# Key norms inside the last projection, transposes first in the chain, and level masks written one level ahead, in a hybrid decoder step

## The chip, the cores and the metric

The kernel runs on one core of a Trainium2 chip. The metric is the device time of one execution in microseconds (us). The kernel before took 2987.66, 2988.45 and 2995.47 us in three runs; the median is 2988.45 us.

One core has five engines that work side by side, each of them strictly in the order in which its own instructions stand: PE (matrix products), DVE and POOL (elementwise work), ACT (activations and copies) and SP, which issues most transfers. An engine that waits for another one holds up everything that stands behind the waiting instruction on it.

## The reference

The program computes one step of a decoder layer over 2048 prompt tokens (with 16 learned tokens ahead of them) and 32 sampling tokens: a layer norm, one projection for two groups of heads, an output projection, and a dense feed-forward net. Four heads are retention heads, four are gated DeltaNet heads. The change lies in the second kind. For each chunk of 128 tokens and each head the reference computes:

```python
gk = l2_norm(silu(conv(...)))                       # keys
G = jnp.cumsum(g, axis=-1)
decay = jnp.exp(jnp.where(incl, G[..., :, None] - G[..., None, :], -jnp.inf))
kk = jnp.einsum('bnhid,bnhjd->bnhij', k, k)
lower = jnp.where(strict, kk * decay, 0.0) * beta[..., :, None]
a_mat = jnp.eye(C, dtype=q.dtype) + lower
sol = lax.linalg.triangular_solve(a_mat, rhs, left_side=True, lower=True, unit_diagonal=True)
attn = jnp.einsum('bnhid,bnhjd->bnhij', q, k) * decay

def step(s, xs):                                    # over the chunks
    wv, wk, at, qg, kt, cd = xs
    u = wv - jnp.einsum('bhcd,bhde->bhce', wk, s)
    o = jnp.einsum('bhcd,bhde->bhce', qg, s) + jnp.einsum('bhij,bhje->bhie', at, u)
    s = cd[..., None, None] * s + jnp.einsum('bhcd,bhce->bhde', kt, u)
    return s, o
```

## The kernel before

The program has three stages one after the other: the mixers of both kinds of heads (`attention`, the first 1310 us or so of the profile), the output projection, and the feed-forward net. The change touches the first stage alone.

**Blocks and heads.** The tokens are worked in four blocks b0 to b3 of four chunks of 128 tokens. Block b0 also has a fifth, short tile, with the learned tokens and the sampling tokens. In each block the eight heads follow in the order r0 g0 r1 g1 r2 g2 r3 g3 (b3: r0 g0 g1 r1 g2 g3 r2 r3), with r a retention head and g a gated DeltaNet head. For each head a projection runs (`ret_proj` or `gdn_proj`): products on PE at line L406, out of `wh`, `wl` (weights, split in a high and a low part) and `xT`, into PSUM tiles `pj`, of which there are two. Behind it the head's chain (`ret_chain` or `gdn_chain`, which calls `gdn_group`) is begun, and its steps are laid between the products of the projections that follow: `advance(us)` is called with the time of each piece of a projection, and takes as many steps of the chain as the list `LAT` and `pace` say. A `yield LAT[i]` in the chain is such a step's end. From what is written in this way, the framework's tile scheduler puts the instructions of each engine in their final order.

**A retention projection** gives q and k of a chunk into one `pj` tile. DVE multiplies it by the rotation's cosines and sines (`qk`, L571, and `rotB`, L572), POOL adds the two (L573, into `qk`), and DVE scales the keys (`rkd`, L634), out of what POOL has added.

**A gated DeltaNet projection** has four parts (q, k, v and the gate), of which each is followed by its short convolution (`cacc`, L862). `flip(a)` (L805 to L820) transposes q or k, takes the square sums of its rows on ACT, and for k leaves the transposed keys in `kp`. Both come in the sixth piece of a part's products: q's in the k part's, k's in the gate part's. The norms' reciprocal square roots and the scale factors `gsk` come when the projection is over.

**The chain of a gated DeltaNet head** (`gdn_group`) begins with the decays: `mg` on DVE (L918), products `pe` with a triangle of ones on PE (L921), the exponential `E` on ACT (L925), and its strict and its inclusive triangle on POOL, `Es` (L926, in `mg`'s buffer, and so named `mg` in the views) and `E` (L927). Then the keys are scaled by `gsk` on DVE (`kp`, L935), v is transposed and scaled (`vb`, L938 and L939), the scaled keys are transposed on PE (L943) and copied by ACT to `kT` (L945), and keys times keys (L949, called kT·kT here) give `LT` on DVE (L951), which is `Es` times that product. From `LT` the triangular matrix is inverted over seven levels: DVE makes the first level's masked matrix `Z` (L960) and `U` (L961), POOL makes the other six, `Lm` (L963), one instruction for each level; then come six rounds of products (L973, L980, L982), each of which uses one slice of `Lm`, and a refinement (L993, L1001). Last comes the scan over the chunks: the products with the state, kS and qS (L1035, L1036), `r` on DVE (L1038), `Vr` on PE (L1043), `ku` (L1052), the state's update on DVE (`S_gdn`, L1053), for which the next chunk's kS waits, and the output `O` (L1055). In b0 a second, small chain (called the side chain here) runs for the short tile between the steps of the first.

**What sets the order.** While the chain of head h runs its inversion, the scan of the same block's previous gated DeltaNet head, which `advance` carries under the key "h", and the retention projection that follows in the head order lie on the same engines. Heads 1 and 2 of a block also have the layer norm of the next block's tokens beside them (`xa` at L307 on DVE and at L309 on POOL).

The lines of the chain's first part, up to the end of the masks, are the ones that the change rewrites:

```python
nc.gpsimd.tensor_tensor(out=Es, in0=E, in1=bc(ST), op=ALU.mult)          # L926
nc.gpsimd.tensor_tensor(out=E, in0=E, in1=bc(M1), op=ALU.mult)           # L927
nc.vector.tensor_tensor(out=kp, in0=kp, in1=lane(sk[:R, 1, here]), op=ALU.mult)   # L935
for x in range(1, nl):
    nc.gpsimd.tensor_tensor(out=Lm[:, x - 1], in0=LT, in1=lvl(x), op=ALU.mult)    # L963
```

Of the kernel before, what the change touches and what calls it, by code (L numbers as in the profile page):

```python
# [239 lines left out]
class Builder:  # L240
# [547 lines left out]
    def gdn_proj(self, b, h, G, out):  # L788
        nc, mp, cp = self.nc, self.mp, self.cvp
        xh, xl = self.xT  # L790
        T = CPB * 128 + (SP if b == 0 else 0)
# [81 lines left out]
        rn = self.rsqrt(sq.rearrange("p a b -> p (a b)"), 2 * nt, 128, self.sm, 1.0, 4.0 * RMS_EPS).rearrange("p (a b) -> p a b", a=2)  # L873
        sk = self.sm.tile([128, 2, nt], F32, tag="gsk", name="gsk")
        nc.vector.tensor_scalar(out=sk[:, 0], in0=rn[:, 0], scalar1=HD ** -0.5, scalar2=None, op0=ALU.mult)
        nc.vector.tensor_tensor(out=sk[:, 1], in0=rn[:, 1], in1=G["sb"][:, :, h], op=ALU.mult)
        out += [cv, zg, sk, kps]
# [20 lines left out]
    def gdn_group(self, b, h, cv, zg, sk, kp, G, mixd, ts, tiles):  # L898
# [21 lines left out]
        for i in range(m):  # L920
            nc.tensor.matmul(pe[:R, i, :R], lhsT=U1, rhs=mg[:, i, :], start=True, stop=True)  # L921
# [6 lines left out]


        kp = kp[:R]  # L930
        vb = big("vb", 2, n=128)[:R]
        lane = lambda a: a.unsqueeze(2).broadcast_to([R, m, 128])
        here = slice(ts[0], ts[0] + m)
        cq = sk[:R, 0, here]
        nc.vector.tensor_tensor(out=kp, in0=kp, in1=lane(sk[:R, 1, here]), op=ALU.mult)  # L935
        p = wide()[:R, :m, :]
        for i in range(m):
            nc.tensor.transpose(p[:, i, :], v[:, col(i):col(i) + R], self.ident)  # L938
        nc.vector.tensor_tensor(out=vb, in0=p, in1=lane(G["sv"][:R, here, h]), op=ALU.mult)  # L939
        yield LAT[7]  # L940
        pk = wide()
        for i in range(m):
            nc.tensor.transpose(pk[:, i, :R], kp[:, i, :], idn)  # L943
        kT = big("kT", 2)[:, :, :R]
        nc.scalar.copy(out=kT, in_=pk[:, 0:m, :R])  # L945
        yield LAT[8]
# [15 lines left out]
        for x in range(1, nl):  # L962
            nc.gpsimd.tensor_tensor(out=Lm[:, x - 1], in0=LT, in1=lvl(x), op=ALU.mult)  # L963
# [695 lines left out]
```

## Time and profile before

| | |
|---|---|
| median of three runs | 2988.45 us (2987.66 to 2995.47) |
| the profiled execution's own time | 2991.86 us |
| span of its instructions | 2990.1 us |
| clock that PE was granted, mean | 0.982 of full speed |
| share of the span that PE is busy | 96% |
| first stage (mixers) | 0 to about 1310 us |
| output projection and feed-forward net | about 1310 us to the end |

The profile shows one execution. "Busy" is the time that an engine's instructions take in the records. A row of grouped instructions gives the line, the engine, the operation, output and inputs with their sizes, the count, then the busy time and the mean nanoseconds of one, and last the idle time just before them with what ended it. A row of waits gives the engine and the line that waited, what it waited for, the total in us, the count, and the longest one. A row of the timeline gives the start in us, the duration, the engine and the line, and in brackets the idle time ahead of it with what ended it. A row of windows gives the stretch and its length, then the busy time (and count) of PE, PE's weight loads, DVE, ACT and POOL, the granted clock, the share of DMA, and GB/s.

### The profile page before, as it was taken

Reading aid. Unit: us, or ns where it says so; the run is one execution under the profiler, and the core shown is the slowest. Engines: PE = TensorE matmul, PEld = TensorE weight load, DVE = VectorE, ACT = ScalarE, POOL = GpSimd, SP = SyncE. Lnnn points to the kernel's source line nnn. Section 1 sums busy time; section 2 is a strip of 40 time slices with the busy share of each in tenths; the row PEclk is TensorE's granted clock in tenths of the full one; section 3 lists DMA queues with packets and bytes.
Section 4 is the critical chain, followed back from the end, with each engine's and each line's share of the span. In section 5 each row is a group of like instructions: output and inputs, shape, how many; then the busy total and the mean of one; then the engine's idle time right before and its main releaser. Section 6 shows DMA issues by size and latency. Waiting matters only on the chain.

```text
span 2990.1 us, 47480 instructions
## 1 busy us (share of the span) xinstructions
PE 2862.8 (96%) x17942; PEld 2554.7 (85%) x17942; DVE 1934.2 (65%) x4205; ACT 996.2 (33%) x2351; POOL 782.9 (26%) x759
## 2 busy tenths in 40 slices
PE   6999999999999999998998999999999999999997
PEld 6877888888888878877777999999999999989895
DVE  7767677776776676657776766667544444844456
ACT  2434343444444444432233333333211112321121
POOL 1312222221222122225544434433200111411111
PEclk8989999999999999999999999999999999999998
DMA  7543534444344333356658766667755555787762
GB/s 258 202 169 142 205 134 152 148 170 152 150 157 156 135 121 122 125 157 228 218 184 286 281 223 228 228 234 260 274 183 184 176 184 184 272 295 238 240 227 85
DMA packets 223093, 580.89 MB, mean 194 GB/s; under 512 B 27296, under 2 KB 62672, under 8 KB 206480
## 3 DMA queue, kind: packets, MB, share of 16 engines
q1 hardware_dynamic: 222864, 577.86, 55.6%
q8 instruction: 141, 2.31, 0.3%
q14 instruction: 88, 0.72, 0.1%
HBM read 409.48 MB, written 168.30 MB: 193 GB/s over the span
## 4 chain that ended last, share of the span: by engine, by line
PE 78%; DVE 13%; DMA 3%; ACT 3%; issue 2%; POOL 1%; SPq 0%; POOLq 0%; ACTq 0%; DVEq 0%
PE d L406 20%; PE pj L406 19%; PE Y L406 8%; PE X L406 8%; PE Z L406 8%; PE W L406 4%; DVE cacc L862 1%; ACT junk L813 1%; PE w L980 1%; DMA bd<-spare 1%; PE rt L668 1%; PE w L973 1%; DMA fr<-bd 1%; PE w L982 1%; PE rt L641 1%
## 5 line engine op out<-in xcount | busy, mean ns | idle before, releaser
L406 PE MATMUL pj<-wh,xT 128*128 128x256 f32 (+2 forms) x2176 | 459.7, 295 | 7.6 <-ACT wh L349 3.7
L406 PE MATMUL pj<-xT,wh 128*128 128x512 f32 (+1 forms) x1280 | 379.7, 381 | 1.8 <-ACT cpre L846 1.0
L406 PEld LDWEIGHTS pj<-wh,xT 128*128 128x128 f32 (+1 forms) x2176 | 353.7, 188 | 12.9 <-ACT wh L349 4.0
L1506 DVE TENSOR_TENSOR y<-y,d 128x512 f32<-128x512 f32 (+1 forms) x344 | 235.2, 684 | 173.6 <-PE d L406 173.5
L406 PE MATMUL pj<-wl,xT 128*128 128x256 f32 (+3 forms) x1088 | 310.6, 286 | 0.5 <-POOL wl L356 0.5
L406 PE MATMUL d<-dh,fh 128*128 128x512 f32 (+1 forms) x745 | 297.4, 399 | 10.1 <-DVE y L1504 6.5
L406 PE MATMUL d<-dh,fl 128*128 128x512 f32 (+1 forms) x745 | 295.5, 397 | 0.0
L406 PE MATMUL d<-dl,fh 128*128 128x512 f32 (+1 forms) x745 | 294.1, 395 | 0.8 <-DVE dl L356 0.8
L356 POOL TENSOR_TENSOR fl<-ta,fh 128x384 fp32r<-128x384 f32 (+1 forms) x65 | 63.8, 981 | 748.7 <-issue 541.5
L406 PEld LDWEIGHTS pj<-xT,wh 128*128 128x128 f32 x1280 | 211.9, 194 | 25.1 <-issue 3.4
L406 PE MATMUL pj<-xT,wl 128*128 128x512 f32 (+1 forms) x640 | 229.7, 359 | 0.0
L406 PEld LDWEIGHTS pj<-wl,xT 128*128 128x128 f32 (+1 forms) x1088 | 205.1, 188 | 1.0 <-POOL wl L356 0.8
L406 PEld LDWEIGHTS d<-dh,fl 128*128 128x128 f32 (+1 forms) x745 | 137.3, 184 | 38.3 <-issue 0.5
L406 PEld LDWEIGHTS d<-dh,fh 128*128 128x128 f32 (+1 forms) x745 | 137.6, 185 | 29.8 <-DVE y L1504 7.1
L406 PEld LDWEIGHTS d<-dl,fh 128*128 128x128 f32 (+1 forms) x745 | 137.5, 185 | 20.6 <-DVE dl L356 1.1
L406 PEld LDWEIGHTS pj<-xT,wl 128*128 128x128 f32 x640 | 122.7, 192 | 16.8 <-issue 0.8
L862 DVE SCALAR_TENSOR_TENSOR cacc<-cpre,cw,cacc 128x512 f32<-128x512 f32 (+1 forms) x144 | 115.9, 805 | 31.9 <-ACT cacc L860 30.4
L963 POOL TENSOR_TENSOR Lm<-LT,lvl 128x512 f16<-128x512 f32 (+1 forms) x108 | 129.2, 1228 | 11.3 <-DVE LT L951 10.5
L1405 DVE TENSOR_TENSOR u<-x,Y 128x384 f32<-128x384 f32 (+1 forms) x132 | 67.6, 512 | 96.3 <-PE Y L406 95.8
L349 ACT CAST fh<-ta 128x384 fp32r<-128x384 f32 (+1 forms) x66 | 31.8, 482 | 289.7 <-DVE ta L1413 289.7
L406 PE MATMUL X<-b,a12h 128*128 128x384 f32 (+1 forms) x528 | 126.2, 325 | 0.4 <-ACT x L1419 0.4
L406 PE MATMUL X<-b,a11h 128*128 128x384 f32 (+1 forms) x528 | 124.7, 321 | 0.0
(391 smaller groups left out, 7170.9 us busy)
## 6 DMA issues: line engine op xcount, KB each, us to landing
wh<-parts SPq DMA_DIRECT2D x45, 1024.0 KB, 5.5
wl<-parts SPq DMA_DIRECT2D x45, 1024.0 KB, 6.8
fr<-dn SPq DMA_DIRECT2D x66, 512.0 KB, 5.6
fr<-gu SPq DMA_DIRECT2D x44, 512.0 KB, 4.9
s12h<-wd SPq DMA_DIRECT2D x44, 512.0 KB, 4.8
s12l<-wd SPq DMA_DIRECT2D x44, 512.0 KB, 5.8
s34h<-wd SPq DMA_DIRECT2D x44, 512.0 KB, 3.8
s34l<-wd SPq DMA_DIRECT2D x44, 512.0 KB, 4.8
```

Of the source, the lines that this page charges most:

```text
L349: i = nc.scalar.copy(out=h, in_=src)
L356: i = (nc.vector if el == "dve" else nc.gpsimd).tensor_tensor(out=l, in0=src, in1=h.bitcast(F32), op=ALU.subtract)
L406: self.nc.tensor.matmul(out, lhsT=a(k), rhs=b(k), start=first and k == 0 and i == 0, stop=last and k == kn - 1 and i == 2, skip_group_chec ...
L641: nc.tensor.matmul(pp[:rows, 2, :rows], lhsT=kT, rhs=qT, start=True, stop=True)
L668: nc.tensor.matmul(po, lhsT=sc, rhs=v, start=True, stop=False)
L813: nc.scalar.activation(out=junk, in_=p[:, j, :], func=AF.Square, accum_out=sq[:, a, t:t + 1])
L862: nc.vector.scalar_tensor_tensor(out=ac, in0=pre[:, i:i + N], scalar=w(i), in1=ac, op0=ALU.mult, op1=ALU.add)
L963: nc.gpsimd.tensor_tensor(out=Lm[:, x - 1], in0=LT, in1=lvl(x), op=ALU.mult)
L973: nc.tensor.matmul(py[:, i, :], lhsT=Lm[:, x - 1, i, :], rhs=T[:, i, :], start=True, stop=True)
L980: nc.tensor.matmul(pt[:, i, :], lhsT=U[:, i, :], rhs=Z[:, i, :], start=True, stop=True)
L1405: add = lambda o, x, p: nc.vector.tensor_tensor(out=o, in0=x, in1=p, op=ALU.add)
L1506: nc.vector.tensor_tensor(out=ys, in0=ys, in1=p, op=ALU.add)
```

## The change

**Key norms.** `norms()` now holds the reciprocal square roots, the factors `gsk` and the scaling of `kp` (now L828). It is called inside the products of the last part, the gate's: in the seventh piece (in b0, the fifth of the second group). `flip(1)` comes earlier, in the first piece of the gate part (in b0, the third of the first group).

**The chain's begin.** It starts with the transposes of the scaled keys (L933) and ACT's copy `kT` (L935), then `mg` (L937) and v's transposes with `vb` (L945, L946). After one step's end come `pe` (L950), the exponential (L953), `Es` and `E` on POOL (L954, L955) and kT·kT (L958) with `LT` (L960), without a step's end between them.

**The masks.** The loop of six `Lm` instructions becomes one for level 1 behind `U`, and one for level x+1 behind the products of level x (now L971). Each still reads only `LT` and a constant.

**The plan's numbers.** `LAT` has two entries fewer, and `INVERSE`, by which `pace` stretches a chain over the projections that follow, goes from 21 to 19.4.

```diff
-LAT = [1.0, 0.7, 0.7, 0.7, 2.0, 0.7, 0.5, 1.2, 1.8, 1.8, 1.0, 1.0, 1.7, 1.0, 0.6, 0.5, 0.5, 1.2]
+LAT = [1.0, 0.7, 0.7, 0.7, 2.0, 0.7, 0.9, 2.8, 1.0, 1.0, 1.7, 1.0, 0.6, 0.5, 0.5, 1.2]
-INVERSE = 21.0
+INVERSE = 19.4
+        def norms():
+
+            rn = self.rsqrt(sq.rearrange("p a b -> p (a b)"), 2 * nt, 128, self.sm, 1.0, 4.0 * RMS_EPS).rearrange("p (a b) -> p a b", a=2)
+            sk = self.sm.tile([128, 2, nt], F32, tag="gsk", name="gsk")
+            nc.vector.tensor_tensor(out=sk[:, 1], in0=rn[:, 1], in1=G["sb"][:, :, h], op=ALU.mult)
+            for kp, ts in zip(kps, sets):
+                r = tiles[ts[0]][0]
+                here = slice(ts[0], ts[0] + len(ts))
+                nc.vector.tensor_tensor(out=kp[:r], in0=kp[:r], in1=sk[:r, 1, here].unsqueeze(2).broadcast_to([r, len(ts), 128]), op=ALU.mult)
+            nc.vector.tensor_scalar(out=sk[:, 0], in0=rn[:, 0], scalar1=HD ** -0.5, scalar2=None, op0=ALU.mult)
+            sks.append(sk)
...
-                        if i == 5 and which % 2 and c0 == groups[-1][0]:
-                            flip(which // 2)
+                        if which == 1 and i == 5 and c0 == groups[-1][0]:
+                            flip(0)
+                        if which == 3 and c0 == 0 and i == (2 if b == 0 else 0):
+                            flip(1)
+                        if which == 3 and c0 == groups[-1][0] and i == (4 if b == 0 else 6):
+                            norms()
...
+        kp = kp[:R]
+        pk = wide()
+        for i in range(m):
+            nc.tensor.transpose(pk[:, i, :R], kp[:, i, :], idn)
+        kT = big("kT", 2)[:, :, :R]
+        nc.scalar.copy(out=kT, in_=pk[:, 0:m, :R])
         mg = big("mg")[:R, :, :R]
         nc.vector.tensor_tensor(out=mg, in0=bc(M1), in1=G["g"][:R, ts[0]:ts[0] + m, h].unsqueeze(2).broadcast_to([R, m, R]), op=ALU.mult)
...
-        for x in range(1, nl):
-            nc.gpsimd.tensor_tensor(out=Lm[:, x - 1], in0=LT, in1=lvl(x), op=ALU.mult)
-        yield LAT[9]
+        masked = lambda x: nc.gpsimd.tensor_tensor(out=Lm[:, x - 1], in0=LT, in1=lvl(x), op=ALU.mult)
+        masked(1)
+        yield LAT[7]
...
+            if x + 1 < nl:
+                masked(x + 1)
```

How the instructions stand on three engines follows; a row has the line, the operation, output and inputs by name and number, and the size; "x6" is six such rows in a row.

**POOL, block b2, the chain of head 0**, with the retention head 1's rotation adds (L573) around it. Before, from the triangles `Es` (L926) and `E` (L927) to the add behind the masks:

```order
L926 TENSOR_TENSOR mg_10072<-E_10085,cb_271 128x512
L927 TENSOR_TENSOR E_10085<-E_10085,cb_271 128x512
L573 TENSOR_TENSOR qk_10166<-qk_10166,rotB_10165 128x256
L573 TENSOR_TENSOR qk_10219<-qk_10219,rotB_10218 128x256
L963 TENSOR_TENSOR Lm_10206<-LT_10204,lvl_273 128x512 x6
L573 TENSOR_TENSOR qk_10264<-qk_10264,rotB_10263 128x256
```

The same place now:

```order
L954 TENSOR_TENSOR mg_10080<-E_10116,cb_271 128x512
L955 TENSOR_TENSOR E_10116<-E_10116,cb_271 128x512
L971 TENSOR_TENSOR Lm_10127<-LT_10125,lvl_273 128x512 x6
L573 TENSOR_TENSOR qk_10180<-qk_10180,rotB_10179 128x256
L573 TENSOR_TENSOR qk_10214<-qk_10214,rotB_10213 128x256
L573 TENSOR_TENSOR qk_10265<-qk_10265,rotB_10264 128x256
```

The six masks, which stood behind the second and third of the four rotation adds, still stand in one row, and now ahead of these two. The same six in a row stand ahead of the adds for head 0 and head 3 of b1 and b2 and for heads 1 and 3 of b3. For heads 1 and 2 of b1 and b2 four masks stand ahead of the second add, and two between it and the third. In b0, where two chains run, the side chain's `Es` and `E` stand behind the six masks of the main one.

**DVE, the same place.** Before, from a `kt` of the scan to the inversion's first `U`:

```order
L571 TENSOR_TENSOR qk_10166<-pj_10118,rott_9069 128x256
L572 TENSOR_TENSOR rotB_10165<-pj_10118,rott_9069 128x256
L1038 SCALAR_TENSOR_TENSOR r_10156<-sc_10161,ng_5963,vb_9127 128x128
L634 TENSOR_SCALAR rkd_10558<-qk_10166,cb_271 128x128
L571 TENSOR_TENSOR qk_10219<-pj_10170,rott_9069 128x256
L572 TENSOR_TENSOR rotB_10218<-pj_10170,rott_9069 128x256
L951 TENSOR_TENSOR LT_10204<-w_10199,mg_10072 128x512
L960 TENSOR_TENSOR Z_10207<-LT_10204,lvl_273 128x512
L1053 SCALAR_TENSOR_TENSOR S_gdn3_301<-S_gdn3_301,eg_5957,sc_10161 128x128
```

Now, from the `Z` behind `LT` to the same update of the state:

```order
L969 TENSOR_TENSOR Z_10128<-LT_10125,lvl_273 128x512
L1064 SCALAR_TENSOR_TENSOR S_gdn3_301<-S_gdn3_301,eg_5963,sc_10069 128x128
L970 SCALAR_TENSOR_TENSOR U_10129<-Z_10128,ident_66 128x512
L1066 SCALAR_TENSOR_TENSOR O_10063<-qs_10067,eg_5963,w_10070 128x128
L1033 TENSOR_SCALAR kt_10251<-kp_8981,eg_5963 128x128
L571 TENSOR_TENSOR qk_10180<-pj_10139,rott_9070 128x256
L572 TENSOR_TENSOR rotB_10179<-pj_10139,rott_9070 128x256
L1049 SCALAR_TENSOR_TENSOR r_10170<-sc_10175,ng_5969,vb_9120 128x128
L634 TENSOR_SCALAR rkd_10556<-qk_10180,cb_271 128x128
L571 TENSOR_TENSOR qk_10214<-pj_10184,rott_9070 128x256
L572 TENSOR_TENSOR rotB_10213<-pj_10184,rott_9070 128x256
L1064 SCALAR_TENSOR_TENSOR S_gdn3_301<-S_gdn3_301,eg_5963,sc_10175 128x128
```

The second `rkd`, which stood ahead of `LT`, now stands behind it, and so behind the masks by way of the second add on POOL; behind it stand the third `qk` and `rotB`, which free the `pj` tile, and a state update. The same order of `rkd`, third `qk`, third `rotB` and state update is found in the chains of b1, b2 and b3 that have rotation adds beside them.

**PE, block b1, the chain of head 1.** Before, the transposes of the scaled keys:

```order
L1052 MATMUL sc_7290<-u_7286,kt_7287 128x128
L1054 MATMUL w_7291<-u_7286,E_6386 128x128
L406 MATMUL pj_7340<-wh_7053,xT_5230 128x256
L406 MATMUL pj_7340<-wl_7054,xT_5230 128x256
L406 MATMUL pj_7340<-wh_7053,xT_5230 128x256 x2
L943 MATMUL w_7359<-ident_66,kp_7216 128x128 x4
```

Now:

```order
L933 MATMUL w_7295<-ident_66,kp_7176 128x128 x4
L945 MATMUL w_7305<-ident_66,post_7140 128x128 x4
L950 MATMUL w_7333<-mg_7302,cb_271 128x128 x4
L958 MATMUL w_7342<-kT_7300 128x128 x4
L406 MATMUL pj_7361<-wh_7053,xT_5236 128x256 x2
L406 MATMUL pj_7361<-wl_7054,xT_5236 128x256
L406 MATMUL pj_7361<-wh_7053,xT_5236 128x256
L1046 MATMUL sc_7397<-S_gdn0_298,kT_6379 128x128
```

The four transposes, which stood 12 instructions behind `pe`, now stand ahead of `pe`, and kT·kT follows at once. Behind this kT·kT 46 projection products (L406), a pair kS and qS, a `Vr`, a pair `ku` and `Eu` and the inversion's first products (L976) stand on PE up to the kS that waits for the state update behind the second `rkd`. In the chains with six masks ahead of the adds (the one of b2 above) it is 66 projection products and one pair more, and for heads 1 and 2 of b0 54 projection products.

More of the change, by code (lines that the diff above doesn't have):

```diff
@@ L818, in flip @@
                     kps.append(kp)
+        def norms():
[8 more added lines that the diff above has]
+            sks.append(sk)
+        sks = []
         for piece in range(2):
@@ L872, in gdn_proj @@
                     cv.append(o)
[L873 to L877, printed above, removed]
+        out += [cv, zg, sks[0], kps]
     def gdn_chain(self, b, h, cvz, G, mixd):
@@ L914, in gdn_group @@
         Ib, Ih, idn = bc(self.ident[:R, :R]), self.identh[:R, :R], self.ident[:R, :R]
+        kp = kp[:R]
[4 more added lines that the diff above has]
+        nc.scalar.copy(out=kT, in_=pk[:, 0:m, :R])
         mg = big("mg")[:R, :, :R]
         nc.vector.tensor_tensor(out=mg, in0=bc(M1), in1=G["g"][:R, ts[0]:ts[0] + m, h].unsqueeze(2).broadcast_to([R, m, R]), op=ALU.mult)
+        vb = big("vb", 2, n=128)[:R]
+        lane = lambda a: a.unsqueeze(2).broadcast_to([R, m, 128])
+        here = slice(ts[0], ts[0] + m)
+        cq = sk[:R, 0, here]
+        p = wide()[:R, :m, :]
+        for i in range(m):
+            nc.tensor.transpose(p[:, i, :], v[:, col(i):col(i) + R], self.ident)
+        nc.vector.tensor_tensor(out=vb, in0=p, in1=lane(G["sv"][:R, here, h]), op=ALU.mult)
+        yield LAT[6]
         pe = wide()
@@ L921, in gdn_group @@
             nc.tensor.matmul(pe[:R, i, :R], lhsT=U1, rhs=mg[:, i, :], start=True, stop=True)
-        yield LAT[6]
         E = big("E", 2)[:R, :, :R]
@@ L927, in gdn_group @@
         nc.gpsimd.tensor_tensor(out=E, in0=E, in1=bc(M1), op=ALU.mult)
[L930 to L946, printed above, removed]
         pl = wide()
@@ L969, in gdn_group @@
         for x in range(1, nl):
-            yield LAT[10]
+            yield LAT[8]
             py = wide()[:R, :m, :R]
@@ L973, in gdn_group @@
                 nc.tensor.matmul(py[:, i, :], lhsT=Lm[:, x - 1, i, :], rhs=T[:, i, :], start=True, stop=True)
+            if x + 1 < nl:
+                masked(x + 1)
             Z = big("Z", 2, F16)[:R, :, :R]
             nc.vector.scalar_tensor_tensor(out=Z, in0=py, scalar=-1.0, in1=Ib, op0=ALU.mult, op1=ALU.add)
-            yield LAT[11]
+            yield LAT[9]
             pt = wide()[:R, :m, :R]
@@ L989, in gdn_group @@
         nc.scalar.copy(out=V, in_=U)
-        yield LAT[12]
+        yield LAT[10]
         pe = wide()[:R, :m, :R]
@@ L997, in gdn_group @@
         for it in range(2):
-            yield LAT[13]
+            yield LAT[11]
             pu = wide()[:R, :m, :R]
@@ L1036, in gdn_group @@
                 nc.tensor.matmul(po[:, 1, :], lhsT=q[:, c0:c0 + R], rhs=S, start=True, stop=True)
-            yield LAT[14]
+            yield LAT[12]
             nc.vector.scalar_tensor_tensor(out=r[:orow], in0=pp[:orow, 0, :], scalar=gc("ng", i, orow), in1=vb[:orow, i, :], op0=ALU.mult, op1=ALU.add)
@@ L1044, in gdn_group @@
             nc.scalar.copy(out=u, in_=pp[:R, 2, :])
-            yield LAT[15]
+            yield LAT[13]
             if sp:
@@ L1059, in gdn_group @@
             nc.scalar.activation(out=junk, in_=O[:orow, i, :], func=AF.Square, scale=cq[:orow, i:i + 1], accum_out=ss[:orow, i:i + 1])
-            yield LAT[16]
+            yield LAT[14]
         rs = self.rsqrt(ss[:orow], m, orow, self.sm, 1.0 / HD, RMS_EPS)
@@ L1064, in gdn_group @@
         nc.vector.tensor_tensor(out=O[:orow], in0=O[:orow], in1=rs.unsqueeze(2).broadcast_to([orow, m, 128]), op=ALU.mult)
-        yield LAT[17]
+        yield LAT[15]
         for i in range(m):
```

## The prediction

> **What bounds the kernel.** I read the page's head first, then windows cut along the blocks of the first stage. The columns of a window: its stretch and length, the busy time of PE, PE's weight loads, DVE, ACT and POOL, the granted clock, DMA's share, GB/s.
>
> ```profile
> span 2990.1 us, 47480 instructions
> PE 2862.8 (96%) x17942; PEld 2554.7 (85%) x17942; DVE 1934.2 (65%) x4205; ACT 996.2 (33%) x2351; POOL 782.9 (26%) x759
> 43.00:470.00 427.00, 406.90 (x3073) 363.55 (x3072) 300.10 (x821) 174.82 (x535) 96.01 (x137) 0.96 0.48 171
> 470.00:1078.00 608.00, 589.18 (x4340) 514.99 (x4339) 425.57 (x1226) 269.18 (x773) 140.78 (x172) 1.00 0.42 154
> 1078.00:1310.00 232.00, 220.10 (x1676) 195.01 (x1674) 155.94 (x404) 105.34 (x299) 55.37 (x68) 0.99 0.33 120
> 1310.00:2990.00 1680.00, 1625.91 (x8758) 1463.59 (x8756) 1015.78 (x1643) 436.61 (x729) 482.99 (x369) 0.99 0.66 223
> ```
>
> PE bounds every stretch: in b0 (43 to 470) it idles 427.0 − 406.9 = 20.1 us, in b1 and b2 18.8, in b3 11.9. The change neither adds nor removes a product. So it can gain at most the idle time that its waits make, out of 51 us in the stage it touches, and it loses whatever new idle time it makes on PE; DVE, busy for 70% of the stage, has slack on the average only. The rest of the kernel, from 1310 us on, is untouched and cancels.
>
> **What is removed.** The view of waits, cut to 43 to 1310 us, has the wait for the scaled keys as a row of its own (total, count, longest), and the timeline of b1, head 1, shows its longest:
>
> ```profile
> PE w L943 <- DVE kp L935: 13.9, 7, 2.6
> 567.97 2.50 POOL L309 TENSOR_TENSOR xa<-xa 128x512 f32<-128x512 f32 x2 [9.45 <-DVE rqt L277]
> 572.96 1.27 DVE L634 TENSOR_SCALAR rkd<-qk,cb 128x128 f32<-128x128 f32 x1
> 574.15 0.68 DVE L935 TENSOR_TENSOR kp<-kp,gsk 128x512 f32<-128x512 f32 x1
> 574.98 0.63 PE L943 MATMUL w<-ident,kp 128*128 128x128 f32 x4 [2.56 <-DVE kp L935]
> ```
>
> The scaling stood behind a `rkd` on DVE, the transposes behind the scaling: 13.9 us in seven places. The scaling now comes within the projection, so in the chains with nothing beside them these transposes find their keys ready. Four of the seven are heads 1 and 2 of b1 and b2, where the next block's layer norm (L307 on DVE, L309 on POOL, 2.50 us for its pair) is put ahead of the norms and the transposes stand earlier on PE than before. For these I keep between 0 and the 2.6 us of the longest wait and take the middle, 1.2 each, 4.8 together. **Removed: 13.9 − 4.8 = 9.1 us.** The earlier `flip(1)` moves transposes and ACT's square sums, which PE does not wait for, within one projection part: counted as 0, with ACT at 42% in this stage as cover. The norms' small operations on DVE are as many as before. The plan's new numbers (`LAT`, `INVERSE` 19.4 for 21) only move steps along the projections; what they move is in the order from which I count below.
>
> **What is added: the masks' new place on POOL.** The masks are written one level ahead, yet still read `LT` alone, so the scheduler keeps them in a row (front of this document, POOL), ahead of the rotation adds L573 instead of behind them. DVE works in order: the second `rkd` (L634) waits for its add, and behind it stand the third `qk` and `rotB`, which free a `pj` tile, and the state update (now L1064) that PE's next kS waits for. So a chain runs masks, add, `rkd`, update, kS. Its prices, by groups (busy, mean ns of one) and one row of the timeline:
>
> ```profile
> L926 POOL TENSOR_TENSOR mg<-E,cb 128x512 f32<-128x512 f32 x16 | 20.7, 1296 | 113.4 <-ACT E L925 102.3 <-DVE rqt L276 11.0
> L927 POOL TENSOR_TENSOR E<-E,cb 128x512 f32<-128x512 f32 x16 | 20.4, 1274 | 0.6
> L925 ACT ACTIVATE E<-w 128x512 f32<-128x512 f32 x16 | 9.5, 597 | 16.0 <-PE w L921 16.0
> L951 DVE TENSOR_TENSOR LT<-w,mg 128x512 f32<-128x512 f32 x16 | 11.0, 690 | 2.6 <-PE w L949 1.3
> 581.71 7.74 POOL L963 TENSOR_TENSOR Lm<-LT,lvl 128x512 f16<-128x512 f32 x6
> L573 POOL TENSOR_TENSOR qk<-qk,rotB 128x256 f32<-128x256 f32 x64 | 48.3, 757 | 158.5 <-DVE rotB L572 139.3 <-DVE rqy L278 10.6 <-PE sc L1052 6.0
> L960 DVE TENSOR_TENSOR Z<-LT,lvl 128x512 f16<-128x512 f32 x16 | 11.7, 729 | 0.5
> L961 DVE SCALAR_TENSOR_TENSOR U<-Z,ident 128x512 f16<-128x512 f16 x16 | 23.2, 1452 | 0.2
> L571 DVE TENSOR_TENSOR qk<-pj,rott 128x256 f32<-128x256 f32 x64 | 26.7, 417 | 34.4 <-PE pj L406 34.3
> L634 DVE TENSOR_SCALAR rkd<-qk,cb 128x128 f32<-128x128 f32 x64 | 21.9, 342 | 10.6 <-POOL qk L573 10.6
> L1053 DVE SCALAR_TENSOR_TENSOR S_gdn<-S_gdn,eg,sc 128x128 f32<-128x128 f32 x64 | 21.9, 342 | 23.8 <-PE sc L1052 23.5
> ```
>
> POOL's order now has `Es` and `E` ahead of the masks, so `LT` and `E` run side by side, both released by `Es`. With time counted from `LT`'s end: `E` ends at 1.27 − 0.69 = 0.58. A mask takes 7.74 / 6 = 1.29. In the chains of heads 1 and 2 of b1 and b2 four masks stand ahead of the second add: 0.58 + 5.16 + 0.76 = 6.5. In those of head 0 of b1 and b2 and of heads 1 and 3 of b3 all six do: 0.58 + 7.74 + 0.76 = 9.1. DVE's own work up to the `rkd` is 3.4 in the first kind (`Z`, `U`, a `qk`, a `rotB`, an `r`) and 4.5 in the second, so DVE stands still for some 3.1 and 4.6 us. Then `rkd`, `qk`, `rotB` and the update take 0.34 + 2 × 0.42 + 0.34 = 1.5: the state is ready at 8.0 and at 10.6.
>
> PE meanwhile: `LT` ends 1.8 us after PE is done with kT·kT, since the decays now start only a step ahead (exponential 0.60 + `Es` 1.30 + `LT` 0.69 = 2.6 behind `pe`, less the 0.8 of kT·kT). The pace of what it has to do comes from the timeline:
>
> ```profile
> 505.26 0.40 PE L406 MATMUL pj<-wh,xT 128*128 128x256 f32 x2
> 505.62 0.40 PE L406 MATMUL pj<-wh,xT 128*128 128x256 f32 x2
> 508.06 1.05 PE L949 MATMUL w<-kT 128*128 128x128 f32 x8
> 508.87 0.36 PE L406 MATMUL pj<-wh,xT 128*128 128x256 f32 x1
> 511.52 0.38 PE L1035 MATMUL sc<-S_gdn,kT 128*128 128x128 f32 x2
> 511.88 0.37 PE L406 MATMUL pj<-wh,xT 128*128 128x256 f32 x1
> ```
>
> Between the first two rows lie three products: 0.12 each. kT·kT takes 508.87 − 508.06 = 0.81, the pair kS and qS 0.36. Up to the kS in question PE has 46 products in the first kind of chain and 66 in the second (front, PE): 46 × 0.12 + 1.1 for two pairs, a `Vr` and the inversion's first products = 6.6, and 66 × 0.12 + 1.4 = 9.3. The state is ready at 1.8 + 8.0 = 9.8 and 1.8 + 10.6 = 12.4. **PE waits 3.2 and 3.1 us, eight times: 25 us.**
>
> In b0 the wait has another way: the side chain's `Es` stands behind the six masks, its `LT` on DVE waits for that, and `rkd` and the state update stand behind it. Heads 1 and 2: 54 × 0.12 + 1.1 = 7.6 of cover; side `LT` at 0.6 + 7.7 + 0.3 (a 48-wide triangle, taken at a quarter of 1.3) = 8.6, the add 9.4, `rkd` 9.7, the update 10.7, and 1.8 before it: 12.5, so 4.9 each. For heads 0 and 3 I did not find how much stands between; 0 to 4.9, the middle of it, 2.4 each. **b0: 14.7 us.** Head 3 of b1 and b2, where the products of the next block's first projection lie between, gets 0 (up to 3.1 each), and heads 0 and 2 of b3, with no rotation adds beside the masks, 0.
>
> **The sum.** 25 + 14.7 − 9.1 = 31, on the profiled execution's own 2991.86 us (span 2990.1) 3023 us; on the median of the runs, 2988.45, it is **3019**.
>
> What speaks for the price is that the same wait exists in a small form before:
>
> ```profile
> DVE rkd L634 <- POOL qk L573: 10.6, 14, 2.0
> 791.02 0.73 POOL L573 TENSOR_TENSOR qk<-qk,rotB 128x256 f32<-128x256 f32 x1 [1.41 <-DVE rotB L572]
> 791.79 0.29 DVE L634 TENSOR_SCALAR rkd<-qk,cb 128x128 f32<-128x128 f32 x1 [0.59 <-POOL qk L573]
> ```
>
> DVE waits for the add even where nothing is ahead of it on POOL, 10.6 us in 14 places, so the `rkd` is not late enough to take six masks. And `rkd` has another trait: 342 ns in the mean, yet 1.27 us at 572.96, when POOL runs `E` beside it:
>
> ```profile
> 572.89 1.26 POOL L927 TENSOR_TENSOR E<-E,cb 128x512 f32<-128x512 f32 x1
> ```
>
> [...]
>
> **The rivals.**
>
> *Covered waits* (the other side: faster). DVE runs ahead of or behind PE by more than I count. The price decides where PE's cover exceeds the chain: a further 3.2 us of products, 27 of them, ahead of the kS. Then only the removed part counts, −9 to −14: 2979 to 2974 on the median. For it: in the kernel before all of PE's waits for DVE in the stage are small beside this, so its plan has reserves, and the scan may stand later than the order's products tell. Against it: the `rkd` stands ahead of the update in every one of these chains, whatever the times.
>
> *Half-covered waits* (no change to little). If the kS in question has some 10 to 20 products more ahead of it than I count, 1.2 to 2.4 us, or if the waits fall in half of the chains only, the added 40 shrink to 8 to 20, and with the 9 to 14 removed the net is −6 to +11: 2982 to 2999. In this case the change doesn't do what its words say: the masks are in a row as before, and only their place has moved.
>
> *The clock falls too* (slower still). What a long idle stretch does to PE is seen at the stage's end:
>
> ```profile
> 574.00:576.00 2.00, 1.02 (x9) 1.05 (x10) 1.54 (x5) 0.36 (x1) 0.15 (x1) 1.00 0.75 250
> 1350.00:1358.00 8.00, 1.09 (x4) 0.72 (x5) 6.66 (x12) 4.79 (x6) 1.52 (x2) 0.64 0.96 361
> 1358.00:1364.00 6.00, 5.98 (x17) 4.82 (x18) 4.91 (x13) 0.67 (x1) 4.18 (x3) 0.62 0.70 201
> ```
>
> After the 2.56 us wait of b1 the clock stays 1.00; after an idle stretch of 6.9 us it is granted at 0.62 for the next 6 us, a loss of 6 × 0.38 = 2.3 us. My waits, 3.1 to 4.9, lie between. Ten of them with 2.3 us each: 3019 + 23 = 3042. [...]
>
> **How the numbers follow.** Forecast (3000 to 3030): 0.50. Clock falls too (3030 to 3045): 0.13. Half-covered (2982 to 2999): 0.19. Covered (2974 to 2979): 0.18. About 0.3%, 9 us, is what a measurement of this kernel tells from no change; so faster 0.18, within it 0.19, slower 0.63. The likeliest gives 3019. The range reaches from 2980, which leaves out the covered case, to 3043, with the bounds of the waits of head 3 and of b0 and most of the clock's case. The forecast's own range is 3000 to 3030.
>
> **What would show it.** In the profile after, the wait of the transposes for `kp` shrinks from 13.9 to under 8. On POOL, rows of six or four `Lm` stand directly ahead of L573, and DVE's wait of `rkd` for L573 grows from 10.6 to some 40 us. A new row, PE's kS waiting for the state update, has some 25 to 40 us, and PE's idle time from 43 to 1310 us goes from 51 to some 80. In b0 DVE's `LT` of the side chain waits for POOL. A clock under 0.95 in the windows of b1 and b2 would speak for the third rival. I am wrong if the masks run ahead of the adds and PE's wait for the update stays under 5 us in all: then PE had more cover than its order shows; or if kT·kT or the transposes wait anew for ACT.

## The result, and the profile after

The changed kernel took 3040.49 us (median of 4 runs, 3038.84 to 3043.48), the kernel before 2988.93 us (4 runs beside it). The ratio is 1.0164, with a 95% interval of 1.0149 to 1.0179: the change costs about 50 us. The profiled execution took 3038.84 us, with a clock of 0.977 in the mean, where it was 0.982.

The head of the page after, and under it, from the windows, the first stage up to the first product of the output projection, first of the kernel before, then of the kernel after (columns as above: stretch, length, busy time of PE, PE's weight loads, DVE, ACT, POOL, clock, DMA share, GB/s):

```profile
span 3037.0 us, 47463 instructions
PE 2870.8 (95%) x17942; PEld 2565.6 (84%) x17942; DVE 1928.6 (64%) x4205; ACT 994.5 (33%) x2351; POOL 784.7 (26%) x759
```

```profile
0.00:1309.90 1309.90, 1236.79 (x9186) 1090.98 (x9187) 918.43 (x2562) 559.58 (x1622) 299.79 (x391) 0.98 0.44 158
```

```profile
0.00:1358.20 1358.20, 1245.08 (x9179) 1100.82 (x9179) 909.91 (x2561) 556.20 (x1618) 299.07 (x391) 0.97 0.42 152
```

The stage got 48.3 us longer, and the span 46.9: all of the loss lies in the stage that the change touches. DVE, ACT and POOL are busy no longer than before; nothing was added to do. PE's idle time grew from 1309.9 − 1236.8 = 73.1 to 113.1 us, 40.0 more, and the same products took 8.3 us more of PE's time.

Where the 40 us are, the view of waits says (waiting engine, tile and line, what it waited for, total us, count, longest). Of the kernel after, PE's largest waits in the stage and what is left of the one removed:

```profile
PE sc L1046 <- DVE S_gdn L1064: 15.9, 12, 2.1
PE sc L1054 <- DVE r L1049: 15.1, 12, 3.1
PE sc L1078 <- DVE O L1075: 7.0, 7, 1.5
PE pj L406 <- DVE LT L960: 6.7, 1, 6.7
PE w L1012 <- DVE rqy L278: 4.3, 3, 3.2
PE pt L525 <- DVE rotB L572: 3.7, 2, 3.5
PE w L976 <- DVE U L970: 3.0, 2, 1.9
PE w L933 <- DVE kp L828: 2.9, 5, 0.7
```

Here L1046 is kS, L1054 the scan's `Vr`, L1078 the transposes of the output, L1012 products of the refinement, L976 the inversion's first products, L933 the transposes of the scaled keys. The wait for the keys fell from 13.9 to 2.9 us, as the change means it to. But PE waits for DVE at kS, at `Vr`, at one `pj` tile and at two transposes of a layer norm (L525) for 41.4 us together, where the kernel before had 2.1 us of these. DVE, in turn, waited for POOL:

```profile
DVE rkd L634 <- POOL qk L573: 44.3, 23, 4.2
...
DVE LT L960 <- POOL mg L954: 26.1, 14, 4.0
```

The first was 10.6 us before, the second did not stand among DVE's waits at all. How both reach PE is seen in the timeline of the chain of b1, head 1 (start, duration, engine, line, and in brackets the idle time ahead). POOL, then DVE, then PE:

```profile
589.50 1.28 POOL L954 TENSOR_TENSOR mg<-E,cb 128x512 f32<-128x512 f32 x1 [0.99 <-ACT E L953]
590.86 1.29 POOL L955 TENSOR_TENSOR E<-E,cb 128x512 f32<-128x512 f32 x1
592.11 5.41 POOL L971 TENSOR_TENSOR Lm<-LT,lvl 128x512 f16<-128x512 f32 x4
597.49 0.73 POOL L573 TENSOR_TENSOR qk<-qk,rotB 128x256 f32<-128x256 f32 x1
```

```profile
590.82 0.69 DVE L960 TENSOR_TENSOR LT<-w,mg 128x512 f32<-128x512 f32 x1 [1.39 <-POOL mg L954]
...
591.75 0.94 DVE L969 TENSOR_TENSOR Z<-LT,lvl 128x512 f16<-128x512 f32 x1
...
592.96 1.30 DVE L970 SCALAR_TENSOR_TENSOR U<-Z,ident 128x512 f16<-128x512 f16 x1
594.18 0.34 DVE L1049 SCALAR_TENSOR_TENSOR r<-sc,ng,vb 128x128 f32<-128x128 f32 x1
598.25 1.16 DVE L634 TENSOR_SCALAR rkd<-qk,cb 128x128 f32<-128x128 f32 x1 [3.73 <-POOL qk L573]
...
600.00 0.33 DVE L1064 SCALAR_TENSOR_TENSOR S_gdn<-S_gdn,eg,sc 128x128 f32<-128x128 f32 x1
```

```profile
594.58 0.49 PE L1054 MATMUL sc<-r,V 128*128 128x128 f32 x2 [1.52 <-DVE r L1049]
...
600.39 0.49 PE L1046 MATMUL sc<-S_gdn,kT 128*128 128x128 f32 x2 [2.11 <-DVE S_gdn L1064]
```

Two delays follow one another. `LT` stands 1.39 us on DVE until POOL has made `Es`; behind it come `Z`, `U` and only then the scan's `r`, for which PE waits 1.52 us. Then DVE stands 3.73 us at `rkd`, because POOL takes four masks ahead of the rotation add; the state update behind it is late, and PE's kS waits 2.11 us.

### The profile page after: what moved, and what is told of

Same layout as the page of the kernel before. It is cut to its first block, busy times and chain, and to the rows that moved or that the text cites. A ratio compares the mean times of both kernels' runs of the same rounds, so it can differ in the third digit from the quotient of the medians.

```text
span 3037.0 us, 47463 instructions
## 1 busy us (share of the span) xinstructions
PE 2870.8 (95%) x17942; PEld 2565.6 (84%) x17942; DVE 1928.6 (64%) x4205; ACT 994.5 (33%) x2351; POOL 784.7 (26%) x759
## 4 chain that ended last, share of the span: by engine, by line
PE 73%; DVE 12%; POOL 5%; DMA 3%; issue 3%; ACT 3%; SPq 0%; POOLq 0%; ACTq 0%; DVEq 0%
PE d L406 19%; PE pj L406 17%; PE Y L406 8%; PE X L406 8%; PE Z L406 8%; PE W L406 4%; POOL Lm L971 3%; POOL mg L954 1%; PE w L982 1%; PE w L991 1%; DVE rqt L272 1%; PE pj L714 1%; DMA bd<-spare 1%; POOL E L955 1%; PE w L993 1%
## 5 line engine op out<-in xcount | busy, mean ns | idle before, releaser
L406 PE MATMUL pj<-wh,xT 128*128 128x256 f32 (+2 forms) x2176 | 462.8, 298 | 14.3 <-DVE LT L960 6.7
L406 PE MATMUL pj<-xT,wh 128*128 128x512 f32 (+1 forms) x1280 | 379.5, 380 | 3.0 <-DVE kp L817 1.3
L406 PEld LDWEIGHTS pj<-wh,xT 128*128 128x128 f32 (+1 forms) x2176 | 358.3, 191 | 17.8 <-issue 6.9
L406 PE MATMUL pj<-wl,xT 128*128 128x256 f32 (+3 forms) x1088 | 313.4, 288 | 0.5 <-POOL wl L356 0.5
L406 PE MATMUL d<-dh,fh 128*128 128x512 f32 (+1 forms) x745 | 297.1, 399 | 10.2 <-DVE y L1515 6.7
L406 PE MATMUL d<-dh,fl 128*128 128x512 f32 (+1 forms) x745 | 295.0, 396 | 0.0
L406 PE MATMUL d<-dl,fh 128*128 128x512 f32 (+1 forms) x745 | 293.5, 394 | 0.8 <-DVE dl L356 0.8
L406 PEld LDWEIGHTS pj<-xT,wh 128*128 128x128 f32 x1280 | 209.8, 193 | 27.9 <-ACT junk L813 4.3
L406 PE MATMUL pj<-xT,wl 128*128 128x512 f32 (+1 forms) x640 | 229.6, 359 | 0.0
L406 PEld LDWEIGHTS pj<-wl,xT 128*128 128x128 f32 (+1 forms) x1088 | 208.6, 192 | 1.2 <-POOL wl L356 0.8
L406 PEld LDWEIGHTS d<-dh,fl 128*128 128x128 f32 (+1 forms) x745 | 137.4, 184 | 38.3 <-issue 0.2
L406 PEld LDWEIGHTS d<-dh,fh 128*128 128x128 f32 (+1 forms) x745 | 137.2, 184 | 29.5 <-DVE y L1515 7.2
L406 PEld LDWEIGHTS d<-dl,fh 128*128 128x128 f32 (+1 forms) x745 | 137.4, 184 | 20.3 <-DVE dl L356 1.1
L406 PEld LDWEIGHTS pj<-xT,wl 128*128 128x128 f32 x640 | 122.3, 191 | 17.6 <-issue 1.1
L971 POOL TENSOR_TENSOR Lm<-LT,lvl 128x512 f16<-128x512 f32 (+1 forms) x108 | 127.9, 1213 | 0.2 <-DVE LT L960 0.2
L406 PE MATMUL X<-b,a12h 128*128 128x384 f32 (+1 forms) x528 | 125.7, 324 | 0.4 <-ACT x L1430 0.4
L406 PE MATMUL X<-b,a11h 128*128 128x384 f32 (+1 forms) x528 | 124.9, 322 | 0.0
```

The costliest lines, as they stand in the source:

```text
L406: self.nc.tensor.matmul(out, lhsT=a(k), rhs=b(k), start=first and k == 0 and i == 0, stop=last and k == kn - 1 and i == 2, skip_group_chec ...
L971: masked = lambda x: nc.gpsimd.tensor_tensor(out=Lm[:, x - 1], in0=LT, in1=lvl(x), op=ALU.mult)
```

## The experiments

Two theories, and a third to be excluded. Theory 1: the masks' place on POOL, ahead of the rotation adds, makes the loss. Theory 2: the decays (`pe`, `E`, `Es`), now laid right ahead of kT·kT, make `LT` late on DVE, and what stands behind it. Theory 3: writing the masks one level ahead makes the loss. Times are medians; ratios are to the kernel before in the same comparison (2988.93 us for the change, 2991.71 us for the next four, 2991.48 us for the last three).

| kernel | what it is | us | ratio (95%) |
|---|---|---|---|
| after | the change | 3040.49 | 1.0164 (1.0149 to 1.0179) |
| after_row | change, masks in a row again | 3051.46 | 1.0203 (1.0188 to 1.0219) |
| after_two | change, masks in two buffers | 3017.39 | 1.0089 (1.0075 to 1.0102) |
| before_norms | before, with early key norms alone | 2975.59 | 0.9952 (0.9940 to 0.9965) |
| before_ahead | before, with masks one level ahead alone | 2987.94 | 0.9996 (0.9985 to 1.0006) |
| after_step | change, one step's end more | 2986.67 | 0.9985 (0.9974 to 0.9996) |
| two_step | both of after_two and after_step | 2991.43 | 0.9998 (0.9986 to 1.0009) |
| norms_two | early norms alone, and masks in two buffers | 2982.43 | 0.9971 (0.9962 to 0.9981) |

**One part at a time: the early key norms.** The kernel before with `norms()` and the earlier `flip(1)`, the scaling taken out of the chain, all else as it was:

```diff
...
+                        if which == 3 and c0 == 0 and i == (2 if b == 0 else 0):
+                            flip(1)
+                        if which == 3 and c0 == groups[-1][0] and i == (4 if b == 0 else 6):
+                            norms()
...
-        nc.vector.tensor_tensor(out=kp, in0=kp, in1=lane(sk[:R, 1, here]), op=ALU.mult)
```

> The kernel before with the key norms and the scaling moved into the last projection part alone; the chain's begin, the masks and the plan's numbers as before. POOL's order is as before. Theories 1 to 3 alike: the 13.9 us of waits for the scaled keys go (down to 0 to 5 us), no new wait comes: 2975 to 2984. A rival (the earlier flip and the norms collide with the projection's own work on DVE and ACT): 2986 to 2995, with new waits of PE for kp or zg.

Measured 2975.59 us, ratio 0.9952 (0.9940 to 0.9965): by the ratio 14 us less. This part of the change does what its words say. That the gain is just the removed wait of 13.9 us is in part chance: in the profile that wait is gone and a new one came (L525 for `zg`, 5.2 us, where there was none), so that PE's idle time in the stage fell by 9.6 us, and its products took 4.0 us less.

**The masks one level ahead, alone.**

```diff
-        for x in range(1, nl):
-            nc.gpsimd.tensor_tensor(out=Lm[:, x - 1], in0=LT, in1=lvl(x), op=ALU.mult)
+        masked = lambda x: nc.gpsimd.tensor_tensor(out=Lm[:, x - 1], in0=LT, in1=lvl(x), op=ALU.mult)
+        masked(1)
...
+            if x + 1 < nl:
+                masked(x + 1)
```

> The kernel before with its masks written one level ahead, and nothing else. Theory 1: POOL's order stays nearly what it was (masks behind the same adds), so 2988 within 5. Theory 3 (writing ahead makes the loss): 3010 to 3040.

Measured 2987.94 us, ratio 0.9996: nothing. The instructions on POOL stand nearly as before, six masks in a row. Theory 3 falls.

**The change with its masks in a row again** (the reverse of that diff, on the changed kernel):

> The changed kernel with its six masks written in one row again, as before the change; key norms and the chain's new begin stay. Theory 1 (the masks' place on POOL ahead of the rotation adds makes the loss, and the new begin of the chain puts them there): six masks now stand ahead of the adds for heads 1 and 2 of b1 and b2 too, where it was four, so two masks more (2.6 us) in four chains: about 3040 + 10 = 3050, between 3040 and 3055. Theory 2 (the decays, now made right ahead of kT.kT, come late; the masks matter little): 3040, within 5. Theory 3 (writing the masks one level ahead makes the loss): back to 2975 to 2995.

Measured 3051.46 us, 11 us more than the change. So under the new begin the masks' writing does matter, and it helps: it leaves four masks instead of six ahead of the second add in four chains. The size is that of theory 1. PE's wait for the state update in those four chains is 3.45 us each, where the change has 2.11; that is 5.4 of the 11 us.

**The change with masks that really wait.** Two buffers make a mask wait for the products two levels before it, so POOL takes two masks (3.18 us in b1, head 1) and then the adds:

```diff
-        Lm = mp.tile([128, nl - 1, m, R], F16, tag=pre + "Lm", name="Lm", bufs=1)[:R]
...
+        def masked(x):
+            Lm[x] = mp.tile([128, m, R], F16, tag=pre + "Lm", name="Lm", bufs=2)[:R]
+            nc.gpsimd.tensor_tensor(out=Lm[x], in0=LT, in1=lvl(x), op=ALU.mult)
```

> The changed kernel with two buffers for the masks instead of six, so that a mask really waits for the products two levels before it, and POOL takes two masks, then the rotation adds. Theory 1: two masks and an add end 0.6 + 2.6 + 0.8 = 4.0 us after LT, about when DVE's own work of 3.4 to 4.5 us is done, so the waits for r and for the state update (31 us) go nearly, and with them most of the 8 us of slower PE: 2985 to 3005, DVE's wait of rkd for the add under 15 us (44.3 in the changed kernel). Theory 2 (late decays): LT stays as late, 3025 to 3040. Theory 3 (writing ahead): no better than 3030.

Measured 3017.39 us: neither theory's number. PE's and DVE's waits say why:

```profile
PE sc L1058 <- DVE r L1053: 15.1, 12, 3.1
PE sc L1082 <- DVE O L1079: 11.4, 7, 2.4
...
PE pj L406 <- DVE LT L960: 2.3, 1, 2.3
```

```profile
DVE rkd L634 <- POOL qk L573: 17.8, 23, 1.5
```

The wait of kS for the state update (15.9 us) is gone from the list, `rkd`'s wait fell from 44.3 to 17.8 us, and the one long wait at a `pj` tile from 6.7 to 2.3: that half was the masks'. The wait of `Vr` for `r` is the same 15.1 us in 12 places, to the tenth: that half is not the masks'.

**The decays a step ahead of kT·kT.** Two edits of a line each to the changed kernel, the second so that the plan's time stays the same:

```diff
         nc.gpsimd.tensor_tensor(out=E, in0=E, in1=bc(M1), op=ALU.mult)
+        yield 1.8
         pl = wide()
...
-LAT = [1.0, 0.7, 0.7, 0.7, 2.0, 0.7, 0.9, 2.8, 1.0, 1.0, 1.7, 1.0, 0.6, 0.5, 0.5, 1.2]
+LAT = [1.0, 0.7, 0.7, 0.7, 2.0, 0.7, 0.9, 1.0, 1.0, 1.0, 1.7, 1.0, 0.6, 0.5, 0.5, 1.2]
```

With the masks in two buffers:

> The changed kernel with two buffers for the masks, and with one step's end more: the decays (pe, E, Es) are laid down a step ahead of kT.kT instead of right ahead of it (1.8 of the plan's 2.8 us go ahead of kT.kT). Theory 2 for the rest (with two buffers alone, 3017 us, LT on DVE still waits for Es on POOL, and r behind LT, Z and U on DVE comes late for PE's Vr: 15.1 us in 12 waits): the waits for r go to under 5 us, and the time to 2990 to 3003. If instead the rest comes from v's transposes, vb or the moved flip: 3012 to 3020 and the same 15 us.

and with the masks as in the change:

> The changed kernel with that one step's end alone, the masks in six buffers as in the change: POOL has six masks ahead of the third and fourth rotation add and none ahead of the second. Theory 1 and 2 together (masks ahead of the adds some 25 us, late decays some 15 to 25 us, each for itself): the masks' part stays at 15 to 25 us, so 3010 to 3030. If the masks' place costs only where LT comes late, both go: under 3000.

Measured 2991.43 and 2986.67 us. In both, `r` and the state update are gone from PE's large waits. With two buffers that is theory 2 as expected. With the masks as in the change it is the second branch of the expectation: both halves of the loss go with this one step's end. Here is what it does on DVE, in the same chain of b1, head 1 (the lines are one higher in this kernel):

```profile
568.77 0.29 DVE L634 TENSOR_SCALAR rkd<-qk,cb 128x128 f32<-128x128 f32 x1 [2.53 <-POOL qk L573]
568.98 0.68 DVE L961 TENSOR_TENSOR LT<-w,mg 128x512 f32<-128x512 f32 x1
569.70 0.69 DVE L970 TENSOR_TENSOR Z<-LT,lvl 128x512 f16<-128x512 f32 x1
570.42 1.54 DVE L971 SCALAR_TENSOR_TENSOR U<-Z,ident 128x512 f16<-128x512 f16 x1
...
572.55 0.33 DVE L1065 SCALAR_TENSOR_TENSOR S_gdn<-S_gdn,eg,sc 128x128 f32<-128x128 f32 x1
```

```profile
569.74 7.73 POOL L972 TENSOR_TENSOR Lm<-LT,lvl 128x512 f16<-128x512 f32 x6 [1.00 <-DVE LT L961]
577.43 1.42 POOL L573 TENSOR_TENSOR qk<-qk,rotB 128x256 f32<-128x256 f32 x2
```

`LT` waits for nothing. `rkd` and, as the order of the program has it, the `r` ahead of it stand in front of `LT` again; the second add on POOL stands in front of the masks. Six masks still take 7.73 us in a row, ahead of the third and fourth adds, but this state update stands on DVE behind no `rkd` that waits for them. DVE still stands at `rkd` for 28.3 us in the stage; only 1.1 us of waits for `r`, and none for a state update, is left among PE's. So the masks' place costs where `LT` comes late and the second `rkd` and the state update stand behind it; six masks in a row alone do not bring the loss.

Not all of the new begin's cost is gone: this kernel is still 11 us above the early norms alone. PE's largest wait in it is a new one, for the inversion's first products (1.3 us in the kernel before, 3.0 in the change):

```profile
PE w L977 <- DVE U L971: 8.7, 11, 1.9
```

Whether that wait makes up the 11 us no run tells apart.

**Both gains together.** The early norms alone, with masks in two buffers:

> The early key norms on the old begin of the chain (2976 us alone), and masks in two buffers, written one level ahead. DVE's wait of rkd for the adds (16.7 us there) falls under 10 us; PE's waits hang on it little, so 2970 to 2977. If a mask that waits for products comes late for the next level's products, PE waits for Lm anew: 2980 or more.

Measured 2982.43 us, above the 2970 to 2977 that I expected, and 7 us more than the early norms alone. It lies where I had put a new wait of PE for `Lm`, but no such wait stands in the view: the number came by another way. `rkd` waits 16.7 us for the adds, as without the two buffers, so the reason that I had for a gain was not there. PE's wait of the output's transposes for `O` is 9.3 us in this kernel and 4.8 us with the norms alone. The same 4.4 to 4.5 us come with the two buffers in the other two pairs: 11.4 against 7.0 (after_two and the change), 11.4 against 6.9 (two_step and after_step). The timeline beside the chain of b1, head 1, shows why. Before `O` is scaled, DVE computes a reciprocal square root in a row of small instructions, which must be done first. With two buffers a mask, now spread out in time, starts on POOL at the same moment as one of them, and that one takes as long as the mask, where with the norms alone it takes 0.16 us:

```profile
596.44 1.15 DVE L277 SCALAR_TENSOR_TENSOR rqt<-rqt,rqa 128x4 f32<-128x4 f32 x1
```

```profile
596.41 1.16 POOL L971 TENSOR_TENSOR Lm<-LT,lvl 128x512 f16<-128x512 f32 x1 [1.88 <-PE w L989]
```

PE's wait for `O` is 1.58 us in this chain and in three like it, where it was 0.43 or 0.44 with the norms alone, which makes the whole difference. So the masks that really wait have a price of their own. The best of the kernels is the early norms alone, ahead of both the kernel before and the change.

## Why the prediction came out as it did

Slower was forecast, by 31 us, and it was some 50: 3040 lies above the 3000 to 3030 that I gave the forecast itself, and inside the wider range. The sign, the place and the chain from the masks to PE's wait held. The clock stood among the rivals only, many small waits were put at nothing, and that the sum of the large waits came out is in part luck.

**Removed waits.** 13.9 − 4.8 = 9.1 us were forecast; measured 13.9 − 2.9 = 11.0. The keys still came late where the layer norm lies beside them, by 0.7 us at most, where I took 1.2.

**The row of masks ahead of the adds.** For a chain of four masks I had, from `LT`'s end: `E` at 0.58, the add done at 6.5, the state at 8.0, DVE standing 3.1 us. In the timeline of b1, head 1, `LT` ends at 591.51, `E` at 592.15 (0.64), the add at 598.22 (6.7), the state update at 600.33 (8.8), and DVE stands 3.73 us. The difference at the end is `rkd`: 1.16 us where I took 0.34, while POOL ran the next two masks (2.26 us from 598.18 on). It took 1.16 us in all four chains of this kind, each time with these two masks on POOL, and 0.28 in the median of the stage; why, the runs do not show. PE's kS waited 2.11 us, not 3.2, since PE had already lost 1.52 us in the same chain to `r`; the two make 3.63.

**What I did not see: `r` behind `LT`.** The prediction's step "`LT` ends 1.8 us after PE is done with kT·kT" has the late decays in it, but I used it only to date the masks. On DVE `r` stands behind `LT`, `Z` and `U`, and PE's `Vr` waits for `r`. The rows of DVE ahead of the prediction show an `r` behind `Z` and `U`; I counted it into DVE's own work and did not ask when PE wants it. That row of waits grew by 15.1 − 1.5 = 13.6 us (`Vr`'s wait after, less before). It does not all come on top of the sum: in the four chains with four masks `Vr` and kS together have the 3.63 us, where I had 3.2 for kS alone, and 6.2 of the 15.1 us are two waits in b0, where I had others. after_two, where it stays to the tenth while the masks' part goes, and after_step, where it goes, show it to be a cause of its own.

**Six masks: over-priced.** For head 0 of b1 and b2 and two heads of b3 I had 3.1 us each. There kS waited 1.37, 1.37, 1.37 and 1.09 us, and `Vr` 0.5 us each. In b1, head 0, the state was ready 10.2 us after `LT`'s end, near my 10.6; but PE had 10.4 us of work of its own ahead of that kS, where I had counted 9.3. So the row of kS, for which I had named 25 to 40 us as a sign, has 15.9.

**b0: the size near by luck, the way another.** I had 14.7 us through the side chain's `LT`, most of it at kS of heads 1 and 2. PE's idle time in b0 grew from 20.1 to 31.9 us. The largest single wait of the stage lies there, 6.7 us, at head 0, put down to that `LT`. But DVE was not idle ahead of it: the main chain's `Z` took 7.88 us (last section). The next, 3.5 us at L525, stands behind a side chain's `Z` that took 3.24 us. Heads 1 and 2 have 3.1 us each at `Vr`, and 1.45 and 0.42 us at kS, where I had 4.9 (by the prices of my own rows the update there is ready at 10.9, not 10.7, and it is 5.1).

**The clock, a rival, came in part, and not where the long waits are.** I had 2.3 us for each of ten waits, 23 us, and gave the case a chance of 0.13. The time came out in that case's 3030 to 3045, but the clock made only a part of it. The windows of the kernel after: around the 6.7 us wait, around two waits of b0 with 3.2 and 3.1 us, and behind two waits of 2.11 us, one of b1 and one of b2:

```profile
119.00:126.00 7.00, 0.33 (x1) 0.36 (x2) 6.96 (x7) 0.00 (x0) 6.32 (x8) 0.66 0.45 172
126.00:133.00 7.00, 7.00 (x40) 6.68 (x40) 2.26 (x7) 0.78 (x2) 2.22 (x6) 0.61 0.01 2
133.00:140.00 7.00, 7.00 (x67) 6.40 (x66) 2.18 (x5) 2.85 (x8) 0.99 (x2) 1.00 0.00 1
192.00:200.00 8.00, 6.46 (x17) 3.80 (x17) 6.30 (x17) 1.39 (x3) 0.00 (x0) 0.50 0.63 240
...
229.00:236.00 7.00, 6.23 (x37) 5.78 (x37) 2.97 (x6) 0.47 (x2) 6.92 (x9) 0.76 0.60 245
...
600.40:604.00 3.60, 3.60 (x32) 3.59 (x33) 2.13 (x6) 1.40 (x5) 1.46 (x3) 1.00 0.36 91
...
974.80:978.00 3.20, 3.16 (x15) 3.16 (x16) 1.84 (x5) 1.23 (x4) 0.78 (x2) 0.50 0.03 5
```

In the 7 us behind the longest wait PE got a clock of 0.61 and did 40 products, and 67 in the 7 us after that at 1.00. Behind the wait of 3.2 us (with two of 0.9 and 1.0 us close after it) it is 0.50, behind the one of 3.1 us 0.76. But behind 2.11 us it is 1.00 in one chain and 0.50 in another, with the same waits on PE. The kernel before has the like, of which the prediction shows only one: its four longest waits for the keys are 2.54 to 2.57 us, and the window behind the one at 860 us has 0.55 (860.4 to 864), behind the other three 1.00. So the length of a wait alone does not decide, and what does is not shown.

Nor do the 8.3 us that PE was busy longer lie behind the long waits of b0. Low clocks stand in b0 in both kernels (0.59 from 192 to 200 us in the kernel before), and PE is busy for 406.9 us of b0 before (43 to 470 us) and 407.1 us after (43 to 482). From b1 to the end of the stage, before and then after:

```profile
470.00:1309.90 839.90, 809.18 (x6013) 709.90 (x6012) 581.51 (x1629) 374.52 (x1072) 196.05 (x239) 0.99 0.40 145
```

```profile
482.00:1358.20 876.20, 817.65 (x6008) 718.08 (x6006) 575.70 (x1627) 368.26 (x1066) 194.25 (x239) 0.98 0.38 139
```

The whole 8.3 us lie here, where no wait is longer than 2.11 us.

**The sum by stage.** Measured: 40.0 us of idle time and 8.3 of slower products, 48.3. Forecast: 39.7 of added waits less 9.1, 31. The four rows named in the first section (kS, `Vr`, the `pj` tile, L525 for `rotB`) grew by 41.4 − 2.1 = 39.3 us, as much as I had added up, though with more in b0 and less in the chains of six masks; the wait for the keys fell by 11.0. All other rows together grew by some 12 us (40.0 + 11.0 − 39.3), in small pieces that I had put at nothing: the refinement's products at L1012 wait 7.9 us, where their like had 4.8, the output's transposes 7.0 for 4.4. These 12 us and the 8.3 of slower products, less the 1.9 that the keys gave beyond my 9.1, are what the forecast lacks.

That the part that was to be gained was gained (14 us, alone) and the loss is the new begin's is shown by one-part kernels; that one step's end, and not the plan's `INVERSE` or the other entries of `LAT`, carries most of it is shown by after_step, which keeps 19.4 and the rest; the 11 us that are left there are open.

## What to carry to other kernels

Where several engines keep a strict order, ask of a chain's step that is pulled together not what it costs, but what the in-order engines will find behind it: here, four instructions laid one behind the other made DVE wait with another chain's work in the queue (1.39 us at `LT`, 3.73 at `rkd`). The masks, made ahead, were only spread out in time where two buffers made them wait; the order in which they are written did not do it (before_ahead, 2987.94 us). Spread out, their writing can meet other work, as `O` showed (PE waits 1.58 us for it, where it was 0.43 or 0.44). And an edit of several parts is to be run part by part: the good one (14 us) was hidden under the bad one (over 60 us).

## What the runs showed of the hardware that was not expected

One DVE instruction, the main chain's `Z`, took 7.88 us, longer than the whole row of six masks that POOL ran beside it (6.71 us). In the kernel after, b0, head 0:

```profile
116.15 7.88 DVE L969 TENSOR_TENSOR Z<-LT,lvl 128x512 f16<-128x512 f32 x1
```

```profile
116.77 6.71 POOL L971 TENSOR_TENSOR Lm<-LT,lvl 128x512 f16<-128x512 f32 x6
```

It began while POOL was still at an add, and ended 0.55 us after the last of six masks. In after_two, where POOL had two masks at that place, the same `Z` took 3.45 us and the masks 2.28, and `Z` again ended 0.55 us after the last mask:

```profile
115.47 3.45 DVE L968 TENSOR_TENSOR Z<-LT,lvl 128x512 f16<-128x512 f32 x1
```

```profile
116.09 2.28 POOL L974 TENSOR_TENSOR Lm<-LT,lvl 128x512 f16<-128x512 f32 x2
```

In after_step, in the same chain, `Z` began 0.05 us ahead of the masks and took 0.69 us, which is its median in the kernel before:

```profile
120.09 0.69 DVE L970 TENSOR_TENSOR Z<-LT,lvl 128x512 f16<-128x512 f32 x1
```

```profile
120.14 8.41 POOL L972 TENSOR_TENSOR Lm<-LT,lvl 128x512 f16<-128x512 f32 x9 [1.00 <-DVE LT L961]
```

In the change, `Z` mostly begins while POOL is at `E`, since `LT` and `E` are released together by `Es`; its median is 1.15 us there, 0.69 before. But in b1 to b3 it took no longer than 0.93 to 1.16 us (0.94 in b1, head 1, where it ended 0.54 us behind `E`, with the masks still to run), and 1.63 to 1.65 us in three heads of b0. Only two were far longer: the one above, and the 48x48 one of the side chain of b0's head 3, which took 3.24 us where its like took 0.72 to 0.86, with masks on POOL beside it:

```profile
435.47 3.24 DVE L969 TENSOR_TENSOR Z<-LT,lvl 48x48 f16<-48x48 f32 x1
```

```profile
436.39 2.96 POOL L971 TENSOR_TENSOR Lm<-LT,lvl 128x512 f16<-128x512 f32 x5
```

What decides this the runs do not tell.
